# One dilated head moved beside another, a closing norm without GpSimd, and one root for four tiles

## The chip, the cores and the metric

One Trainium2 chip, one of its cores. The metric is the device time of one execution in microseconds (us). A core has five engines that run side by side: TensorE (PE in the profile; PEld are its weight loads), VectorE (DVE), ScalarE (ACT), GpSimd (POOL) and SyncE (SP), whose queue issues nearly all DMA transfers here. On-chip memory is SBUF (128 partitions) and PSUM (eight banks, where TensorE writes).

## What is computed

The reference runs two transformer blocks, one after the other, on 1024 tokens of width 1024. The first block (two attentions and a mixture of experts) ends about half way and is not touched. The second block, cut to what matters here:

```python
h = _rmsnorm(x, norm_attn_g) * (1.0 + sc1) + sh1              # opening norm
proj = h @ w_in
y_attn = _dilated_attention(q_a, k_a, v_a, rel_bias)           # 8 heads, three branches each
y_delta = _gated_deltanet(q_d, k_d, v_d, z_d, ...)             # 8 heads, a recurrence over chunks
x = x + g1 * (concatenate([y_attn, y_delta]) @ w_out)
h = _rmsnorm(x, norm_ffn_g) * (1.0 + sc2) + sh2
x = x + g2 * ((silu(h @ w_gate) * (h @ w_up)) @ w_down)
return _rmsnorm(x, final_norm_g)                               # closing norm
```

A norm is `x * rsqrt(mean(x*x) + eps) * g`. A dilated head has three branches: (window 128, dilation 1), (512, 4) and (2048, 16).

## The kernel before

Tokens are cut into eight tiles of 128 rows. Matrix products are done in three passes on operands split into a high and a low part (`mm3`). Each tile of data has a tag in a pool, and a pool has a number of buffers (`bufs`) for each tag; a new tile of a tag waits until an older one is released. A pool that is opened later may lie over the space of a closed one, and then its tiles wait for the old tiles under them. The order of the instructions on each engine is not written by hand: the framework (`TileContext(..., schedule_with_timeline_sim=True)`) replays a modelled timeline at build time and gives an engine whatever is ready in it, earlier program text first. On the chip each engine and the SP queue then run in that order.

**Opening norm** (`norm_rows`, L1381). The eight tiles are loaded (L2065) and normed in two groups of four, and each group in two pairs: ScalarE squares and sums each tile (L1390), `rsqrt_small` takes the root of the pair on VectorE in 13 small dependent instructions (L68 to L80), and VectorE and ScalarE scale one tile each (L1393). Then TensorE transposes the four tiles block by block (L1397), ScalarE applies the modulation (L1399), and the high and low parts are made (L1400, L1401; mostly VectorE).

**Dilated heads and recurrence** (`mix`, L1986). Heads 0 to 3 are computed earlier. Then come, in program text, the recurrence of the delta rule (L2145 to L2153; pool `t7` for its tiles, PSUM pool `psE` with two banks `dm` and one bank `ch`) and heads 4 to 7 (L2157). The heads use PSUM pool `psD`: two banks `sc` for scores, two banks `tr` for transposes, one bank `ov` for the product with the values. One head (`dilated_head`, L1524) goes through ten rounds: four of branch 1, four of branch 4, two of branch 16. A round is: score matmuls (L1529, L1530), bias and row minimum on VectorE (`soft`, L1533), exponential on ScalarE (L1534), transposes on TensorE (L1575, L1604 to L1606, L1630), a split into high and low parts that reads the transpose bank (`split`, L1543 to L1548), and the product with the values (`pv`, L1552 to L1554). Results leave through `dl_o2` (L1584) and `dl_on` (L1614, L1637; one buffer, so the third branch waits until the store of the second one, L1616, has landed). Heads 4 and 6 keep their operands in other places (`second`) than heads 5 and 7 (`t6`), but the biases `db1`, `db4`, `db16` have one place each, so that those of head 7 are loaded (L2039 to L2043) when head 6 has used its own. The working tiles (`dl_p`, `at_ph` and so on) are shared by all heads.

**After the heads** (`out_2`, L2163). The eight row blocks of `w_out` are loaded into three raw buffers (tag `big`, L2188), multiplied by the gate on GpSimd (L2189), and split by ScalarE and VectorE (L2190, L2191); the operands are split into `oA` (L2198, L2199), which lies over the operand places of head 7. In the program's memory layout the three raw buffers lie over the recurrence's `dt_nn` (bytes 59680 to 71967 of a partition against 62464 to 74751), and the split weights (`woh`, from byte 84512) lie over its `dt_wq`, `dt_z`, `dt_v` and `dt_zz`.

**Closing norm** (`ffn`, L2340 to L2354). The groups are tiles 0 to 2, 3 to 5, and 6 with 7. ScalarE squares, `rsqrt_small` takes the root, then an odd tile is scaled by VectorE in one instruction (L2350) and an even tile by ScalarE and GpSimd in two (L2352, L2353), and each tile is stored whole (L2354).

Of the kernel before, what the change touches and what calls it, by code (L numbers as in the profile page):

```python
# [6 lines left out]
F32 = mybir.dt.float32  # L7
F32R = mybir.dt.float32r
BF16 = mybir.dt.bfloat16
I32 = mybir.dt.int32  # L10
ALU = mybir.AluOpType
AF = mybir.ActivationFunctionType
AX = mybir.AxisListType
P = 128
T = 1024
D = 1024
# [4 lines left out]
EPS = 1e-6  # L21
# [10 lines left out]
class SplitPool:  # L32


    def __init__(self, a, na, b, nb):
        self.pools = [a] * na + [b] * nb
        self.n = {}

    def tile(self, shape, dt, tag=None, name=None, bufs=None):
        i = self.n[tag] = self.n.get(tag, -1) + 1  # L40
        return self.pools[i % len(self.pools)].tile(shape, dt, tag=tag, name=name)


class TagPool:
# [5 lines left out]
    def tile(self, shape, dt, tag=None, name=None, bufs=None):  # L50
        if tag in self.tags:
            pool, tag, bufs = self.tags[tag]
            return pool.tile(shape, dt, tag=tag, name=name, bufs=bufs)
        return self.main.tile(shape, dt, tag=tag, name=name, **({} if bufs is None else dict(bufs=bufs)))

# [7 lines left out]
def rsqrt_small(C, pool, out, x, n, scale, eps):  # L63

    nc = C.nc
    rows = x.shape[0]
    v = pool.tile([rows, n], F32, tag=f"rs_v{n}", name="rs_v")
    nc.vector.tensor_scalar(v, x, scale, eps, ALU.mult, ALU.add)  # L68
    i0 = pool.tile([rows, n], I32, tag=f"rs_i{n}", name="rs_i")
    nc.vector.tensor_scalar(i0, v.bitcast(I32), 1, None, ALU.logical_shift_right)  # L70
    y0 = pool.tile([rows, n], I32, tag=f"rs_y{n}", name="rs_y")
    nc.vector.tensor_scalar(y0, i0, -1.0, 1597463007.0, ALU.mult, ALU.add)
    nc.vector.tensor_scalar(v, v, -0.5, None, ALU.mult)
    y = y0.bitcast(F32)
    a = pool.tile([rows, n], F32, tag=f"rs_a{n}", name="rs_a")
    for it in range(3):
        nc.vector.tensor_mul(a, y, y)
        nc.vector.tensor_mul(a, a, v)
        dst = out if it == 2 else y
        last = nc.vector.scalar_tensor_tensor(dst, a, 1.5, y, ALU.add, ALU.mult)  # L80
    return last.ins
# [1299 lines left out]
def norm_rows(C, pool, xs, psp, a_col, s_col, ht):  # L1381

    nc = C.nc
    for g in range(2):
        for t2 in (4 * g, 4 * g + 2):
            ss = pool.tile([P, 2], F32, tag="nt_ss", name="nt_ss", bufs=2)
            rstd = pool.tile([P, 2], F32, tag="nt_r", name="nt_r", bufs=2)
            for j in range(2):
                junk = pool.tile([P, D], BF16, tag="nt_junk", name="nt_junk", bufs=2)
                nc.scalar.activation(junk, xs[t2 + j], AF.Square, accum_out=ss[:, j:j + 1])  # L1390
            rsqrt_small(C, pool, rstd, ss, 2, 1.0 / D, EPS)
            for j in range(2):
                (nc.scalar.mul if j else nc.vector.tensor_scalar_mul)(xs[t2 + j], xs[t2 + j], rstd[:, j:j + 1])  # L1393
        for k in range(KD):
            pt = psp.tile([P, 512], F32, tag=C.ps_tag, name="pt", bufs=C.ps_bufs)
            for j in range(4):
                nc.tensor.transpose(pt[:, j * P:(j + 1) * P], xs[4 * g + j][:, k * P:(k + 1) * P], C.ident)  # L1397
            full = pool.tile([P, 512], F32, tag="nt_full", name="nt_full", bufs=3)
            nc.scalar.activation(full, pt, AF.Identity, bias=s_col[:, k:k + 1], scale=a_col[:, k:k + 1])  # L1399
            (nc.scalar.copy if k % 4 == 3 else nc.vector.tensor_copy)(ht.hi[g][:, k], full)  # L1400
            nc.vector.tensor_sub(ht.lo[g][:, k], full, ht.hi[g][:, k])  # L1401
# [584 lines left out]
def mix(C, I, xtile, xclose, km, ext_d, c2_col, x2_d):  # L1986
    nc, tc = C.nc, C.tc
# [8 lines left out]
    num_d, f_d = mk("num_d", [3, 512, T]), mk("f_d", [3, 8, T])  # L1996
    yT_d = mk("yT_d", [512, T])
    w = I["w_in_2"][0]
    with ExitStack() as es:
# [31 lines left out]
                    yield  # L2031
        extra = iter(())

        def head(h, tp):
            qs = load_stack(C, tp, qa_d[h], "at_q")
            ks = load_stack(C, tp, ka_d[h], "at_k")
            kw = load_stack(C, tp, ka_d[h], "at_kw", swap=True)
            b1 = tp.tile([P, 256], F32, tag="db1", name="db1", bufs=1)
            nc.sync.dma_start(b1, toeplitz(ext_d, h, 0, P, 256, 127))  # L2039
            b4 = tp.tile([P, 256], F32, tag="db4", name="db4", bufs=1)  # L2040
            nc.sync.dma_start(b4, toeplitz(ext_d, h, 1, P, 256, 127))
            b16 = tp.tile([P, P], F32, tag="db16", name="db16", bufs=1)
            nc.sync.dma_start(b16, toeplitz(ext_d, h, 2, P, P, 255))  # L2043
            vh = va_d[:, h]
            v1 = tp.tile([P, NT, P], F32R, tag="dv1", name="dv1", bufs=1)
            nc.sync.dma_start(v1.bitcast(F32), vh.rearrange("(t p) c -> p t c", p=P))
            v4 = tp.tile([P, 4, 2, P], F32R, tag="dv4", name="dv4", bufs=1)
            v4s = vh.rearrange("(b j r) c -> j r b c", r=4, b=2)
            for r in range(4):
                nc.sync.dma_start(v4[:, r].bitcast(F32), v4s[:, r])  # L2050
            v16 = tp.tile([P, 8, P], F32R, tag="dv16", name="dv16", bufs=1)
            nc.sync.dma_start(v16.bitcast(F32), vh.rearrange("(j r) c -> j r c", r=8))
            dilated_head(C, tp, psp, qs, ks, kw, v1, v4, v16, b1, b4, b16, mn[:, h], rs[:, h], num_d, h,
                         lambda: next(extra, None))
        with ExitStack() as es2:
            ent2 = es2.enter_context
# [3 lines left out]
            with tc.tile_pool(name="t3", bufs=1, reuse_waits="tile") as tp:  # L2060
                ht = HT(C, ht_pool, "ht")
                xs = []
# [68 lines left out]
        with tc.tile_pool(name="t7", bufs=1, reuse_waits="tile") as td, \  # L2131
                tc.tile_pool(name="t8", bufs=1, reuse_waits="tile", side="right") as t8, \
                tc.tile_pool(name="psE", bufs=1, space=bass.MemoryType.PSUM, reuse_waits="tile") as psr:
            reserve(td, [("dt_yt", [P, 512], 2), ("dt_o", [P, 512], 2)])
            zs = []
            for nm in ("D", "V", "N"):
                zs.append([])
                for i in range(2):
                    z = td.tile([P, 8, P], F32, tag=f"z{nm}{i}", name="z" + nm)
                    nc.gpsimd.memset(z, 0.0)  # L2140
                    zs[-1].append(z)
            S = td.tile([P, 4, P], F32, tag="S", name="S")
            nc.gpsimd.memset(S, 0.0)
            inv, res = {}, {}
            for t in range(NT + 2):  # L2145
                if t < NT:
                    inv[t] = delta_inverse(C, td, psr, t, *zs, zT_d, U_d, T_d, V_d, qk_d, nat_d, qg_d)
                if 0 < t <= NT:
                    got = delta_chain(C, td, psr, t - 1, G, S, *inv.pop(t - 1))
                if t > 1:  # L2150
                    delta_out(C, td, psr, *res.pop(t - 2), yT_d)
                if 0 < t <= NT:
                    res[t - 1] = delta_sum(C, td, psr, *got)  # L2153
            second = TagPool(tp, dict(at_q=(posts, "cv_x", 2), at_k=(posts, "cv_x", 2), at_kw=(posts, "cv_y", 2),
                                      dv1=(posts, "cv_y", 2), dv4=(t8, "dv4", 1), dv16=(t8, "dv16", 1)))
            extra = first_half(TagPool(t8, dict(mr=(posts, "vp_nat", 2))))
            for h in range(4, 8):  # L2157
                head(h, second if h % 2 == 0 else tp)
        right.close()
    return dict(mn=mn, rs=rs, num_d=num_d, f_d=f_d, dil_d=dil_d, yT_d=yT_d, x2_d=x2_d)  # L2160

# [127 lines left out]
def ffn(C, I, y, ht, es, psp, out):  # L2289
    nc, tc = C.nc, C.tc  # L2290
# [10 lines left out]
    for g0 in range(0, NF, GS):  # L2301
# [30 lines left out]
        for t in range(NT):  # L2332
            st = slice(t * P, t * P + P)
            for nh in range(2):
# [2 lines left out]
                for f in fs:  # L2337
                    mm3(nc, ps, av[f][0][:, st], av[f][1][:, st], dw[f][0][:, ns], dw[f][1][:, ns], f == fs[0], f == fs[-1])
                nc.vector.tensor_add(y[t][:, ns], ps, y[t][:, ns])  # L2339
    for ts in ((0, 1, 2), (3, 4, 5), (6, 7)):  # L2340
        n = len(ts)
        ss = tp.tile([P, n], F32, tag="f_ss", name="f_ss", bufs=2)
        r = tp.tile([P, n], F32, tag="f_r", name="f_r", bufs=2)
        for j, t in enumerate(ts):
            junk = tp.tile([P, D], BF16, tag="sg", name="f_junk", bufs=2)
            nc.scalar.activation(junk, y[t], AF.Square, accum_out=ss[:, j:j + 1])
        rsqrt_small(C, tp, r, ss, n, 1.0 / D, EPS)
        for j, t in enumerate(ts):
            if t % 2:
                nc.vector.scalar_tensor_tensor(y[t], y[t], r[:, j:j + 1], fg, ALU.mult, ALU.mult)  # L2350
            else:
                nc.scalar.mul(y[t], y[t], r[:, j:j + 1])  # L2352
                nc.gpsimd.tensor_mul(y[t], y[t], fg)  # L2353
            nc.sync.dma_start(out[0, t * P:(t + 1) * P], y[t])  # L2354


def all_consts():
# [93 lines left out]
```

## Time and profile before

| what | us |
|---|---|
| median of 3 runs | 3562.4 |
| lowest and highest run | 3549.02, 3568.53 |
| the profiled execution, its own time | 3557.78 |
| its span, first to last instruction | 3556.0 |
| opening norm, first square to first product | 1885.65 to 1914.76 |
| heads 6 and 7, and what is left of the recurrence | about 2612 to 2685 |
| last `ps_dn` matmul of the kernel | about 3536.6 |

All times of rows are counted from the span's start. The span is one execution; its own time lies 1.78 us over its span and 4.6 us under the median. Busy shares are means over the whole span, so a stage is read from its own stretch.

### The profile page before, as it was taken

The page shows a single profiled execution, that of the slowest core. Times are in us where ns is not written, and L with a number is a line of the kernel's source. Part 1 is how long each engine was busy: PE and PEld are TensorE (multiplying, and loading weights), DVE is VectorE, ACT ScalarE, POOL GpSimd, SP SyncE. Part 2 cuts the span into 40 slices and gives each one's busy share as a digit, 9 for nine tenths or more (in the row PEclk, how much of TensorE's full clock was granted, in tenths as well). Part 3 has the DMA queues.
Part 4 walks back from the last instruction along what each step waited for, and adds up shares of the span by engine and source line. Part 5 has one row for each costly group of instructions (what it writes and reads, how often), then busy time and mean ns, then how long its engine had stood idle before and what let it go on. Part 6 is the DMA issues. An engine that isn't in the chain of part 4 may idle for free. (4 is left out here: it accounts for less than half of the span.)

```text
span 3556.0 us, 45053 instructions
## 1 busy us (share of the span) xinstructions
PE 3206.1 (90%) x15623; PEld 2529.3 (71%) x15623; DVE 2153.5 (61%) x4635; ACT 1408.2 (40%) x2610; POOL 705.3 (20%) x493
## 2 busy tenths in 40 slices
PE   7997898988879699999996988899998899999997
PEld 4866676766668466666665775688986788888886
DVE  5779895578657865666645676584776633333333
ACT  4345654555322344545434533265552311111112
POOL 0000033234242011111100000012233242322321
PEclk9998899998989799999997998899988999999999
DMA  6553535446564698999964566847665221111111
GB/s 202 124 163 83 156 115 160 132 143 202 178 204 165 252 304 320 336 336 343 332 218 148 155 202 212 195 139 222 181 189 187 68 77 42 54 48 42 54 36 48
DMA packets 442693, 601.38 MB, mean 169 GB/s; under 512 B 91081, under 2 KB 299097, under 8 KB 442464
## 3 DMA queue, kind: packets, MB, share of 16 engines
q1 hardware_dynamic: 433248, 581.17, 51.6%
q0 software_dynamic: 9216, 17.33, 2.0%
q8 instruction: 124, 2.03, 0.2%
q14 instruction: 105, 0.86, 0.1%
HBM read 498.78 MB, written 120.55 MB: 174 GB/s over the span
## 5 line engine op out<-in xcount | busy, mean ns | idle before, releaser
L246 ACT CAST wh<-wr 128x1024 fp32r<-128x1024 f32 (+1 forms) x392 | 379.2, 996 | 333.4 <-PE ps_gu L270 131.0
L250 DVE TENSOR_TENSOR wl<-wr,wh 128x1024 fp32r<-128x1024 f32 (+1 forms) x324 | 365.1, 1155 | 130.5 <-ACT wh L246 122.4
L269 PE MATMUL ps_gu<-hh,wh 128*128 128x512 f32 x704 | 274.7, 392 | 0.0
L270 PE MATMUL ps_gu<-hl,wh 128*128 128x512 f32 x704 | 274.1, 390 | 0.0
L271 PE MATMUL ps_gu<-hh,wl 128*128 128x512 f32 x704 | 273.9, 390 | 0.0
L269 PE MATMUL ps_feat<-hh,wh 128*128 128x512 f32 x640 | 266.6, 417 | 0.1
L270 PE MATMUL ps_feat<-hl,wh 128*128 128x512 f32 x640 | 261.1, 408 | 0.0
L271 PE MATMUL ps_feat<-hh,wl 128*128 128x512 f32 x640 | 260.7, 407 | 0.0
L1328 PE MATMUL ps_y<-wr,at 128*128 128x512 f32 x512 | 235.1, 614 | 24.9 <-ACT at L1322 24.9
L544 POOL TENSOR_TENSOR at_pl<-at_pf,at_ph 128x384 fp32r<-128x384 f32 (+1 forms) x96 | 91.6, 955 | 681.3 <-DVE at_ph L543 641.3
L2321 DVE TENSOR_TENSOR sg<-ps_gu,sg 128x512 f32<-128x512 f32 x44 | 30.4, 692 | 302.3 <-PE ps_gu L271 302.2
L269 PE MATMUL ps_e<-wh,xh 128*128 128x512 f32 x512 | 202.2, 402 | 1.2 <-ACT xh L1301 1.2
L2339 DVE TENSOR_TENSOR y<-ps_dn,y 128x512 f32<-128x512 f32 x176 | 120.7, 690 | 131.7 <-PE ps_dn L271 131.5
L270 PE MATMUL ps_e<-wl,xh 128*128 128x512 f32 x512 | 199.5, 397 | 0.0
L1328 PEld LDWEIGHTS ps_y<-wr,at 128*128 128x128 f32 x512 | 97.2, 195 | 143.0 <-issue 109.1
L271 PE MATMUL ps_e<-wh,xl 128*128 128x512 f32 x512 | 196.1, 397 | 2.4 <-DVE xl L1302 2.4
L250 POOL TENSOR_TENSOR wl<-wr,wh 128x1024 fp32r<-128x1024 f32 (+1 forms) x68 | 155.8, 2292 | 189.0 <-ACT wh L246 188.9
L161 DVE SCALAR_TENSOR_TENSOR adaacc<-adar,c,adaacc 128x512 f32<-128x512 f32 x140 | 118.6, 847 | 98.5 <-DMA adar<-in_w_ada 53.5
L526 ACT ACTIVATE at_p<-at_p,at_mn 128x128 f32<-128x128 f32 (+7 forms) x128 | 99.2, 776 | 185.9 <-DVE at_mn L524 185.7
L269 PE MATMUL ps_tok<-wh,hh 128*128 128x512 f32 (+2 forms) x448 | 169.7, 379 | 0.7 <-DVE hh L237 0.4
L270 PE MATMUL ps_tok<-wl,hh 128*128 128x512 f32 (+2 forms) x448 | 167.7, 374 | 0.0
L271 PE MATMUL ps_tok<-wh,hl 128*128 128x512 f32 (+2 forms) x448 | 166.7, 375 | 0.0
(622 smaller groups left out, 8175.2 us busy)
## 6 DMA issues: line engine op xcount, KB each, us to landing
wr<-in_exp_w SPq DMA_DIRECT2D x384, 512.0 KB
adar<-in_w_ada SPq DMA_DIRECT2D x96, 256.0 KB
wr<-in_w_in SPq DMA_DIRECT2D x44, 512.0 KB
adar<-in_ada_w SPq DMA_DIRECT2D x64, 256.0 KB
wr<-in_w_gate SPq DMA_DIRECT2D x22, 512.0 KB
wr<-in_w_up SPq DMA_DIRECT2D x22, 512.0 KB
dr<-in_w_down SPq DMA_DIRECT2D x22, 512.0 KB
wr<-in_w_in SPq DMA_DIRECT2D x40, 256.0 KB
```

Source lines behind the costliest of these rows:

```text
L161: nc.vector.scalar_tensor_tensor(acc, wt, c_col[:, k:k + 1], acc, ALU.mult, ALU.add)
L246: nc.scalar.copy(hi, raw)
L250: (nc.vector if eng[1] == "v" else nc.gpsimd).tensor_sub(lo, raw, hi)
L269: nc.tensor.matmul(out, sth, mvh, start=start, stop=False)
L270: nc.tensor.matmul(out, sth, mvl, start=False, stop=False)
L271: nc.tensor.matmul(out, stl, mvh, start=False, stop=stop)
L526: nc.scalar.activation(pr[:, :L], pr[:, :L], AF.Exp, bias=mn[:, nch - 1:nch], scale=-1.0, accum_out=rsum[:, qb:qb + 1])
L544: nc.gpsimd.tensor_sub(pl[:, off:], pf[:, off:], ph[:, off:])
L1328: nc.tensor.matmul(po, at[:, k], pcs2[k][:, ns], start=k == 0, stop=k == 3)
L2321: nc.vector.tensor_mul(s, pss[1], s)
L2339: nc.vector.tensor_add(y[t][:, ns], ps, y[t][:, ns])
```

## The change

Three edits. The opening norm takes one root for the four tiles of a group, and the squares of every second tile go to VectorE. Head 7 gets `work`, a pool that puts its working tiles into the places of the recurrence's tiles, and `banks`, which puts its scores and its transposes into the two `dm` banks and its value product into the `ch` bank; its operands and biases stay where they were. Its `dl_on` has two places in turn (`zD0`, `zV0`). The closing norm scales all tiles in one VectorE instruction each, tile 6 has its own root, and tile 7 is squared, scaled and stored in two halves.

```diff
+class CyclePool:
+    def __init__(self, main, tags):
+        self.main, self.tags, self.n = main, tags, {}
+    def tile(self, shape, dt, tag=None, name=None, bufs=None):
+        if tag in self.tags:
+            i = self.n[tag] = self.n.get(tag, -1) + 1
+            pool, tag, bufs = self.tags[tag][i % len(self.tags[tag])]
+            return pool.tile(shape, dt, tag=tag, name=name, bufs=bufs)
...
 (norm_rows)
-        for t2 in (4 * g, 4 * g + 2):
-            ss = pool.tile([P, 2], F32, tag="nt_ss", name="nt_ss", bufs=2)
...
-                nc.scalar.activation(junk, xs[t2 + j], AF.Square, accum_out=ss[:, j:j + 1])
-            rsqrt_small(C, pool, rstd, ss, 2, 1.0 / D, EPS)
+        for j in range(4):
+            junk = pool.tile([P, D], BF16, tag="nt_junk", name="nt_junk", bufs=2)
+            if j % 2:
+                nc.vector.scalar_tensor_tensor(junk, xs[4 * g + j], 1.0, xs[4 * g + j], ALU.mult, ALU.mult,
+                                               accum_out=ss[:, j:j + 1])
+            else:
+                nc.scalar.activation(junk, xs[4 * g + j], AF.Square, accum_out=ss[:, j:j + 1])
+        rsqrt_small(C, pool, rstd, ss, 4, 1.0 / D, EPS)
...
 (mix)
-            dilated_head(C, tp, psp, qs, ks, kw, v1, v4, v16, b1, b4, b16, mn[:, h], rs[:, h], num_d, h,
+            dilated_head(C, work or tp, banks or psp, qs, ks, kw, v1, v4, v16, b1, b4, b16, mn[:, h], rs[:, h], num_d, h,
...
-            for h in range(4, 8):
+            behind = lambda *tags: [(td, tag, bufs) for tag, bufs in tags]
+            work = CyclePool(td, dict(dl_p=behind(("dt_z", 3), ("dt_zz", 2), ("dt_u", 2)), at_ph=behind(("dt_v", 2)),
+                                      at_pl=behind(("dt_wq", 2)), dl_f=behind(("dt_vn", 2)), dl_p16=behind(("dt_nn", 2)),
+                                      dl_o2=behind(("dt_qk", 2)), dl_on=behind(("zD0", 1), ("zV0", 1))))
+            banks = TagPool(psp, dict(sc=(psr, "dm", 2), tr=(psr, "dm", 2), ov=(psr, "ch", 1)))
+            for h in range(4, 7):
                 head(h, second if h % 2 == 0 else tp)
+            head(7, tp, work, banks)
...
 (ffn)
-    for ts in ((0, 1, 2), (3, 4, 5), (6, 7)):
+    for ts in ((0, 1, 2), (3, 4, 5), (6,), (7,)):
+        n, parts = len(ts), 2 if ts == (7,) else 1
+        w = D // parts
...
+        if parts == 2:
+            nc.vector.tensor_add(ss[:, 0:1], ss[:, 0:1], ss[:, 1:2])
...
-            if t % 2:
-                nc.vector.scalar_tensor_tensor(y[t], y[t], r[:, j:j + 1], fg, ALU.mult, ALU.mult)
-            else:
-                nc.scalar.mul(y[t], y[t], r[:, j:j + 1])
-                nc.gpsimd.tensor_mul(y[t], y[t], fg)
-            nc.sync.dma_start(out[0, t * P:(t + 1) * P], y[t])
+            for q in range(parts):
+                c = slice(q * w, (q + 1) * w)
+                nc.vector.scalar_tensor_tensor(y[t][:, c], y[t][:, c], r[:, j:j + 1], fg[:, c], ALU.mult, ALU.mult)
+                nc.sync.dma_start(out[0, t * P:(t + 1) * P, c], y[t][:, c])
```

## Rows read from the trace of the kernel before

**Rows 1.** The page: busy time by engine, and the chain's shares by engine.
```profile
PE 3206.1 (90%) x15623; PEld 2529.3 (71%) x15623; DVE 2153.5 (61%) x4635; ACT 1408.2 (40%) x2610; POOL 705.3 (20%) x493
...
PE 31%; DMA 6%; DVE 6%; ACT 1%; issue 1%; SPq 1%; POOL 0%; POOLq 0%; DVEq 0%; ACTq 0%
```

**Rows 2.** Stretches, opening norm: length, PE, PEld, DVE, ACT, POOL busy, clock, DMA.
```profile
1885.00:1897.00 12.00, 3.35 (x12) 2.15 (x12) 7.22 (x42) 10.89 (x19) 0.00 (x0) 0.50 1.05 394
1897.00:1909.00 12.00, 7.51 (x28) 5.13 (x29) 12.00 (x31) 11.06 (x15) 0.00 (x0) 0.50 0.34 91
```

**Rows 3.** Order in time on ScalarE, opening norm: start, duration, instruction, idle before.
```profile
1889.56 1.06 ACT L1390 ACTIVATE nt_junk<-wr 128x1024 bf16<-128x1024 f32 x1
...
1896.85 1.43 ACT L1399 ACTIVATE nt_full<-pt,sh,a 128x512 f32<-128x512 f32 x2
```

**Rows 4.** Order in time on VectorE: first and last instruction of one root.
```profile
1888.12 0.17 DVE L68 TENSOR_SCALAR rs_v<-nt_ss 128x2 f32<-128x2 f32 x1 [13.47 <-DMA wr<-x_d]
...
1890.30 0.16 DVE L80 SCALAR_TENSOR_TENSOR nt_r<-rs_a,rs_y 128x2 f32<-128x2 f32 x1
```

**Rows 5.** Busy time by stretch, heads 6 and 7 (columns as in Rows 2).
```profile
2629.00:2685.00 56.00, 47.77 (x326) 43.86 (x326) 38.52 (x122) 36.77 (x112) 27.40 (x20) 0.80 0.55 170
2671.00:2685.00 14.00, 7.55 (x65) 6.25 (x66) 10.40 (x11) 7.74 (x11) 6.25 (x5) 0.81 0.33 90
```

**Rows 6.** The chain that ended last, in time, where head 7 ends.
```profile
2678.39 2.90 DMA num_d<-dl_on
...
2683.55 3.71 DMA wr<-in_w_out
```

**Rows 7.** Order in time on TensorE, last value products of head 7.
```profile
2678.42 0.28 PE L1552 MATMUL po<-dl_ph,dv 128*64 128x128 f32 x1 [1.63 <-ACT dl_on L1614]
...
2682.53 0.37 PE L1552 MATMUL po<-dl_ph,dv 128*64 128x128 f32 x1 [3.17 <-DVE dl_on L1637]
```

**Rows 8.** Order in time on the SP queue: head 7's biases, branches 1 and 16.
```profile
2624.99 0.90 SPq L2039 DMA_DIRECT2D db<-ext_d  x1
...
2645.01 0.32 SPq L2043 DMA_DIRECT2D db<-ext_d  x1
```

**Rows 9.** Order in time: head 7's first reduction, then a later round.
```profile
2644.90 0.29 DVE L1533 CUSTOM_DVE_ANT_0 dl_p<-ps_d,db 128x128 f32<-128x128 f32 x1
...
2651.59 0.51 PE L1575 MATMUL pt<-ident,dl_p 128*128 128x128 f32 x3
...
2651.86 0.36 PE L1529 MATMUL ps_d<-at_k,at_q 128*128 128x256 f32 x1
...
2652.96 0.42 DVE L1533 CUSTOM_DVE_ANT_0 dl_p<-ps_d,db 128x256 f32<-128x256 f32 x1
...
2653.48 0.56 DVE L1548 TENSOR_TENSOR dl_pl<-pt,dl_ph 128x384 fp32r<-128x384 f32 x1
```

**Rows 10.** Order in time on GpSimd, the gate on one row block.
```profile
2687.39 2.48 POOL L2189 TENSOR_TENSOR wr<-wr,g1b 128x1024 f32<-128x1024 f32 x1 [7.88 <-DMA wr<-in_w_out]
```

**Rows 11.** Order in time on VectorE, closing norm.
```profile
3534.51 1.83 DVE L70 TENSOR_SCALAR rs_i<-rs_v 128x3 int32<-128x3 int32 x1
...
3541.69 2.30 DVE L68 TENSOR_SCALAR rs_v<-f_ss 128x2 f32<-128x2 f32 x1
...
3546.20 1.29 DVE L2350 SCALAR_TENSOR_TENSOR y<-y,f_r,fgb 128x1024 f32<-128x1024 f32 x1
```

**Rows 12.** The chain that ended last, in time, closing norm.
```profile
3540.76 3.21 POOL y L2353
...
3547.45 2.38 POOLq L2447
```

**Rows 13.** Busy time by stretch, closing norm (columns as in Rows 2).
```profile
3524.00:3537.00 13.00, 12.58 (x56) 10.09 (x54) 10.99 (x28) 7.56 (x12) 4.80 (x2) 1.00 0.20 81
3537.00:3556.00 19.00, 0.00 (x0) 0.00 (x0) 9.86 (x26) 3.33 (x4) 5.54 (x2) 0.58 0.42 166
```

**Rows 14.** Order in time on the SP queue, the eight stores.
```profile
3531.73 18.45 SPq L2354 DMA_DIRECT2D out<-y  x8
```

More of the change, by code (lines that the diff above doesn't have):

```diff
@@ L52, in tile @@
             pool, tag, bufs = self.tags[tag]
+            return pool.tile(shape, dt, tag=tag, name=name, bufs=bufs)
+        return self.main.tile(shape, dt, tag=tag, name=name, **({} if bufs is None else dict(bufs=bufs)))
+class CyclePool:
[5 more added lines that the diff above has]
+            pool, tag, bufs = self.tags[tag][i % len(self.tags[tag])]
             return pool.tile(shape, dt, tag=tag, name=name, bufs=bufs)
@@ L1384, in norm_rows @@
     for g in range(2):
-        for t2 in (4 * g, 4 * g + 2):
-            ss = pool.tile([P, 2], F32, tag="nt_ss", name="nt_ss", bufs=2)
-            rstd = pool.tile([P, 2], F32, tag="nt_r", name="nt_r", bufs=2)
-            for j in range(2):
-                junk = pool.tile([P, D], BF16, tag="nt_junk", name="nt_junk", bufs=2)
-                nc.scalar.activation(junk, xs[t2 + j], AF.Square, accum_out=ss[:, j:j + 1])
-            rsqrt_small(C, pool, rstd, ss, 2, 1.0 / D, EPS)
-            for j in range(2):
-                (nc.scalar.mul if j else nc.vector.tensor_scalar_mul)(xs[t2 + j], xs[t2 + j], rstd[:, j:j + 1])
+        ss = pool.tile([P, 4], F32, tag="nt_ss", name="nt_ss", bufs=2)
+        rstd = pool.tile([P, 4], F32, tag="nt_r", name="nt_r", bufs=2)
+        for j in range(4):
[6 more added lines that the diff above has]
+        rsqrt_small(C, pool, rstd, ss, 4, 1.0 / D, EPS)
+        for j in range(4):
+            (nc.scalar.mul if j % 2 else nc.vector.tensor_scalar_mul)(xs[4 * g + j], xs[4 * g + j], rstd[:, j:j + 1])
         for k in range(KD):
@@ L2032, in mix, with head @@
         extra = iter(())
-        def head(h, tp):
+        def head(h, tp, work=None, banks=None):
             qs = load_stack(C, tp, qa_d[h], "at_q")
@@ L2339, in ffn @@
                 nc.vector.tensor_add(y[t][:, ns], ps, y[t][:, ns])
-    for ts in ((0, 1, 2), (3, 4, 5), (6, 7)):
-        n = len(ts)
-        ss = tp.tile([P, n], F32, tag="f_ss", name="f_ss", bufs=2)
+    for ts in ((0, 1, 2), (3, 4, 5), (6,), (7,)):
+        n, parts = len(ts), 2 if ts == (7,) else 1
+        w = D // parts
+        ss = tp.tile([P, n * parts], F32, tag="f_ss", name="f_ss", bufs=2)
         r = tp.tile([P, n], F32, tag="f_r", name="f_r", bufs=2)
         for j, t in enumerate(ts):
-            junk = tp.tile([P, D], BF16, tag="sg", name="f_junk", bufs=2)
-            nc.scalar.activation(junk, y[t], AF.Square, accum_out=ss[:, j:j + 1])
-        rsqrt_small(C, tp, r, ss, n, 1.0 / D, EPS)
-        for j, t in enumerate(ts):
-            if t % 2:
-                nc.vector.scalar_tensor_tensor(y[t], y[t], r[:, j:j + 1], fg, ALU.mult, ALU.mult)
-            else:
-                nc.scalar.mul(y[t], y[t], r[:, j:j + 1])
-                nc.gpsimd.tensor_mul(y[t], y[t], fg)
-            nc.sync.dma_start(out[0, t * P:(t + 1) * P], y[t])
+            for q in range(parts):
+                junk = tp.tile([P, w], BF16, tag="sg", name="f_junk", bufs=2)
+                nc.scalar.activation(junk, y[t][:, q * w:(q + 1) * w], AF.Square, accum_out=ss[:, j + q:j + q + 1])
+        if parts == 2:
+            nc.vector.tensor_add(ss[:, 0:1], ss[:, 0:1], ss[:, 1:2])
+        rsqrt_small(C, tp, r, ss[:, 0:n], n, 1.0 / D, EPS)
+        for j, t in enumerate(ts):
+            for q in range(parts):
+                c = slice(q * w, (q + 1) * w)
+                nc.vector.scalar_tensor_tensor(y[t][:, c], y[t][:, c], r[:, j:j + 1], fg[:, c], ALU.mult, ALU.mult)
+                nc.sync.dma_start(out[0, t * P:(t + 1) * P, c], y[t][:, c])
 def all_consts():
```

## The prediction

> **What bounds the kernel now.** First the page: TensorE is busy 90% of the span, and the largest share of the chain that ended last, 31%, is its own [rows 1]. That invites the reading that only TensorE's work counts, and none of the three edits removes TensorE work. So the next view is the busy time by stretch, at the places of the edits.
>
> In the opening norm TensorE is busy 3.35 of 12 us at first [rows 2]; the reader is to see that ScalarE (10.89 of 12, then 11.06) leads and VectorE (7.22, then 12.00) takes over. The bound here is the chain from the loads through squares, root and scaling to the first transposed part. In heads 6 and 7 TensorE is busy 47.77 of 56 us: it leads, with 8.23 us idle, of which 6.45 lie in the last 14 us [rows 5]. The order in time on TensorE says what the idle time there is: 1.63 and 3.17 us ahead of the last value products [rows 7], and the chain says why: a store of `dl_on` of 2.90 us that the third branch waits for [rows 6]. In the closing norm TensorE is busy 12.58 of 13 us and then not at all for 19 us [rows 13]; whatever shortens those 19 us shortens the run one for one.
>
> **Opening norm.** Removed: four of eight ScalarE squares of 1.06 us [rows 3] and two of four roots. A root is 13 dependent operations from 1888.12 to 1890.46, 2.34 us [rows 4]. Added: four squares on VectorE. No such instruction is in the rows; the nearest is the scaling of the same form and size, 1.29 us [rows 11], and I take 1.25, with 1.06 (ScalarE's) and 1.46 (as far above) as bounds. Chain for the first group: the fourth tile's square can start at 1889.56, as now [rows 3]; 1.25 on VectorE ends at 1890.8, the root at 1893.2, and two scalings on each engine, at ScalarE's 1.06 a tile, at about 1895.3. Some 0.5 for the last tile's transpose, and the first transposed part is taken up at 1895.8; now it is at 1896.85 [rows 3]. So I take −1.0. If the removed root's whole 2.34 comes off, −2.3; if the framework puts two VectorE squares of the second group (2 x 1.25) into the first group's root, +2.5. VectorE, at 12.00 of 12 later in the stage, is why I don't take the full gain. The shift carries into the first product, which waits for the group's transposes.
>
> **Heads 6 and 7.** Nothing is removed; a dependency is. Head 7 now begins when head 6's last scores leave the banks, at 2644.90 [rows 9]. Its first bias (one place, free since head 6 used its own) is issued from 2624.99 on for 0.90 [rows 8]; with a transfer of 2.90 like the store's [rows 6] it has landed at 2628.8. The recurrence has left its banks by about then, so 2629 is the earliest start. The bias of branch 16 was issued at 2645.01 [rows 8], and still needs head 6's to be used first: only branches 1 and 4 can move much. TensorE's work is the same. What can be won is idle time: 8.23 us [rows 5]. With two heads to draw on and two places of `dl_on` I fill all of it: −8.2. Of the clock the row says 0.80 granted [rows 5], so 40% of the stretch at 1.2 GHz and the rest at 2.4. Fewer gaps may raise it; I take 0.86, 47.77 x (1 − 0.80/0.86) = −3.3, with bounds 0.80 (0) and 0.92 (−6.2).
>
> On the other side, the places move a cost downstream. The raw buffers of `w_out` lie over `dt_nn`, where head 7 keeps `dl_p16` until its end, and the split weights over its other places. Before, three row blocks are loaded and gated ahead of head 7's end; after, they follow it. Each is 2.48 us on GpSimd [rows 10], so up to 7.4 us is uncovered, plus a load of 3.71 [rows 6] that other loads overlap. But the fourth block's load starts only at 2683.55 even now [rows 6], and the product needs the six following blocks too; head 7 ends earlier by the gain, and the blocks catch up. I take +2, bounds 0 and +7.4. The SP queue carries head 7's stores and then these loads; an earlier head moves both.
>
> The banks: head 7 has two for scores and transposes where the others have four. Score start to last reduction's end is 2651.86 to 2653.38, 1.5 us; transposes to the split's end 2651.59 to 2654.04, 2.45 us [rows 9]. Taken in turn, each kind has one bank, so rounds cannot be closer than 2.45: ten are 24.5 us, 2629 to 2654, ahead of the bias of branch 16 or near it. So the banks cost nothing while they only take turns; fully serial, 4.0 us a round, is the rival below. Sum: −8.2 − 3.3 + 2 = −9.5, rounded to −9; bounds −14.4 (−8.2 − 6.2) and, from the rival, +11.
>
> **Closing norm.** Removed: GpSimd's scalings, 3.21 on the chain and 2.38 just before its last link [rows 12], and ScalarE's. VectorE stalls while GpSimd runs: 1.83 and 2.30 us [rows 11] for small root operations of 0.17 elsewhere [rows 4], 3.8 us together. Added on VectorE: four scalings of 1.29 [rows 11], one root (2.3 us alone, about 1.5 among other work) and one small add. VectorE is busy 10.99 + 9.86 = 20.85 us in the last 32 us [rows 13]; 20.85 − 3.8 + 5.2 + 1.6 = 23.8. It was idle half of the last 19 us, so it has room, but becomes the tail's bound. After the last addition, at about 3537, the new path is a half square (half of ScalarE's 1.06, twice, overlapped with the product's end), add, root 2.3, two half scalings of 0.65, and a half store. VectorE's queue ends at 3546.5 to 3548.4; now the last store is issued at 3550.18, the end of the eight stores' group [rows 14], and lands 5.8 us later. So the issue comes 2 to 3.5 us earlier and the half-size store lands perhaps 0.7 earlier: −3.5; bounds −5.5 (VectorE's 23.8 without a gap, from 3524) and −0.5 (every saved microsecond queued on VectorE).
>
> [...] The row that carries the largest term is TensorE's 47.77 busy of 56, with weight loads at 43.86 in the same stretch [rows 5]. [...]
>
> **The rivals.** Sum for the forecast: −1.0 − 9 − 3.5 = −13.5 on the profiled 3557.78, or 3544.3; that execution is 4.6 us under the median, and the run is compared with medians, so 3549.
> - *Forecast*, 3543 to 3555.
> - *A: more room on TensorE.* Its records overlap, so a busy stretch can take more. For: weight loads leave 12.1 us [rows 5]. Against: both rows count the same 326 instructions on one array, and a matmul's own time is part of it. −1.0 − (12.1 + 3.3 − 2) − 3.5 = −17.9: 3544.5; with the clock's bounds 3541 to 3548.
> - *B: slower.* Place: the two `dm` banks. Scores and transposes of one round hold both and the next waits for the whole round: 4.0 us unloaded, and in a stretch where TensorE and VectorE serve two heads 1.4 times that, 5.6. It decides from 5.2 us a round on, (2685 − 4 − 2629)/10: head 7 then ends no earlier than now. At 5.6 it ends 4 later, and the uncovered gating of `w_out` adds 7.4: +11.4 − 4.5 = +6.9, 3569; at 7 us a round 3583. For: `dl_p` rounds hold banks through VectorE, busy 38.5 of 56, and ScalarE, 36.8 [rows 5]. Against: the two kinds take turns, as said.
> - *C: the gain goes.* Head 7 starts early, but what ends the stretch stays: the branch of dilation 16 waits for its bias, and the gated weights come as late as now. Heads 0, other edits −4.5: 3558. For: the fourth block at 2683.55 [rows 6]. Against: the 4.8 us of waits [rows 7] go in any case.
>
> The Trainium skill ("Perfetto Trace Analysis", section "Optimizing Tensor Performance") says that independent matmul groups should rotate through different PSUM banks so that emptying one overlaps the next; head 7 rotates through half as many, which is B's side, and by it the time would be B's 3569.
>
> **How the numbers follow.** Chances: forecast 0.42, A 0.25, B 0.19, C 0.14. The predicted time is 3549. The range: from 3533 (every term at its best: −2.3 − 14.4 − 5.5 = −22.2 gives 3540, and the run spread of before reaches 13 us under its median, of which I take half) to 3573 (B's 3569 and some). About 0.07 lies below, 0.10 above. 0.5% is 17.8 us, about what a measurement of this kernel can tell from no change, as single runs spread over 19.5 us. Faster means under 3544.6: of the forecast 0.3 of its chance (its lower end and the spread), of A most (0.8): 0.33. Slower means over 3580: B's far end, 0.09. Same: 0.58.
>
> **What would show it.** Head 7's first reduction near 2630 and not 2644.9; its last store before 2680; the waits of 1.63 and 3.17 gone; a stretch 2629 to 2675 with TensorE busy over 93% and a granted clock over 0.80; the `w_out` loads bunched behind head 7. Against: reductions of head 7 over 5 us apart (B), or the first products of `out_2` where they were (C). Opening: the first modulated part near 1895.9. Tail: no GpSimd, no VectorE operation of 0.17 that takes 2 us, last store issued near 3547, 16 us from the last product to the end where it was 19.4. The prediction fails if the replayed order, which every edit changes, puts other work ahead in stages between 1900 and 3524 that no edit touches.

## The result and the profile after

The changed kernel takes 3582.6 us (median of 10), the kernel before 3555.6 in the runs beside it: ratio 1.0082, 95% interval 1.0070 to 1.0094. It is slower by 27 us (medians) or 29 (the ratio); the prediction said 3549 and left 0.09 for slower. Its profiled execution has a span of 3582.4 us, 26.4 more than before.

The page after, busy time by engine and the chain's shares, beside [rows 1]:

```profile
PE 3211.2 (90%) x15623; PEld 2532.3 (71%) x15623; DVE 2163.3 (60%) x4636; ACT 1403.2 (39%) x2600; POOL 695.7 (19%) x489
...
PE 31%; DMA 7%; DVE 6%; issue 2%; ACT 1%; SPq 1%; POOL 1%; DVEq 0%; POOLq 0%; ACTq 0%
```

TensorE has the same 15,623 instructions and 5 us more busy time: 21 of the 26 us are idle time. Where it lies is read by cutting both spans at six landmarks: the first square of the opening norm, the first product `ps_tok`, the first product of the recurrence (`ps_z`), the last output tile of the recurrence (`dt_yt`), the last evacuation of head 7 (`dl_on`), and the last `ps_dn`. Each entry is the difference of two such times, in us:

| stretch | before | after | change |
|---|---|---|---|
| opening norm | 29.1 | 32.2 | +3.1 |
| to the recurrence | 511.0 | 509.8 | −1.2 |
| recurrence (with heads 4 to 6) | 222.5 | 229.2 | +6.7 |
| rest of heads 6 and 7 | 36.9 | 45.6 | +8.7 |
| end of the heads to the last product | 851.3 | 870.3 | +19.0 |
| closing norm | 19.4 | 14.7 | −4.7 |

The remaining −5.0 lies ahead of the first square (1885.7 before, 1880.7 after), in work that no edit touches. Busy time by stretch after, for head 7, for what follows it, and for the end (length, PE, PEld, DVE, ACT, POOL, granted clock, DMA), beside [rows 5, 13]:

```profile
2651.00:2697.00 46.00, 35.36 (x212) 29.17 (x211) 20.83 (x65) 24.89 (x76) 11.86 (x10) 0.71 0.30 82
2697.00:2709.00 12.00, 2.20 (x14) 1.43 (x13) 2.35 (x3) 3.11 (x5) 3.82 (x2) 0.64 0.82 282
3555.00:3568.00 13.00, 12.75 (x57) 10.23 (x55) 11.39 (x27) 5.42 (x9) 0.00 (x0) 1.00 0.30 121
3568.00:3582.40 14.40, 0.00 (x0) 0.00 (x0) 10.86 (x46) 1.53 (x6) 0.00 (x0) 0.63 0.46 182
```

Head 7 leaves TensorE idle for 10.6 of 46 us at a granted clock of 0.71, and behind the head TensorE works 2.2 of 12 us. VectorE's order in time, head 7's first and last reductions after, beside the first line of [rows 9]:

```profile
2651.16 0.67 DVE L1999 TENSOR_TENSOR dt_yt<-pt_y,dt_z 128x512 f32<-128x512 f32 x1
2651.76 0.27 DVE L1550 CUSTOM_DVE_ANT_0 dl_p<-ps_d,db 128x128 f32<-128x128 f32 x1
...
2684.31 0.29 DVE L1550 CUSTOM_DVE_ANT_0 dl_p<-ps_d,db 128x128 f32<-128x128 f32 x1 [2.57 <-PE ps_d L1547]
...
2689.03 0.28 DVE L1550 CUSTOM_DVE_ANT_0 dl_p<-ps_d,db 128x128 f32<-128x128 f32 x1
```

Head 7 doesn't start earlier: its first reduction stands right behind the recurrence's last `dt_yt`, which reads the last output tile, transposed into `pt_y`, out of a `dm` bank. TensorE, in order of time there:

```profile
2649.99 0.60 PE L1997 MATMUL pt_y<-ident,dt_o 128*128 128x128 f32 x4
2650.35 0.31 PE L1546 MATMUL ps_d<-at_k,at_q 128*128 128x128 f32 x1
```

Head 7's first scores come right behind the transposes `pt_y`, and before `dt_yt` reads these out (2651.16), so they go into the other `dm` bank. The recurrence's last tile there, `ps_i`, had been read by 2632.46: that bank had been empty for some 18 us. So no full bank held head 7; its place in TensorE's order, behind `pt_y`, did, and why the framework put it there isn't shown. And from its first to its last reduction it takes 37.6 us; before it took 23.2 (2644.90 to 2668.13). The SP queue after, behind the head:

```profile
2697.46 0.45 SPq L1655 DMA_DIRECT2D num_d<-dl_on  x1
2697.95 0.58 SPq L2201 DMA_DIRECT2D g1b<-rg  x1
...
2699.26 0.39 SPq L2211 DMA_DIRECT2D wr<-in_w_out  x1
```

The first load of `w_out` is issued 1.8 us behind head 7's last evacuation; before it was issued 30.1 us ahead of it (2655.14 against 2685.25). TensorE after, in order of time:

```profile
2696.12 2.73 PE L1669 MATMUL pt_w<-ident,dmn 128*4 128x128 f32 x16
2708.65 1.65 PE L283 MATMUL ps_o<-woh,oA 128*128 128x512 f32 x3 [9.80 <-ACT woh L2213]
```

It waits 9.80 us for the first split block. So about half of the 19 us is lost before the first product ends, 12.0 us behind the head where it was 2.1. The other half builds up over the stage: loads, gates and splits that lay under head 7 now stand beside the products, and the first transposes of the next norm come 121.0 us behind the head where they came at 102.9. Groups of instructions on VectorE, 2697 to 2733 after (busy us, mean ns of one):

```profile
L2222 DVE TENSOR_TENSOR oA<-mo,oA 128x512 fp32r<-128x512 f32 x8 | 12.5, 1583 | 11.4 <-ACT oA L2221 11.4
L2214 DVE TENSOR_TENSOR wol<-wr,woh 128x1024 fp32r<-128x1024 f32 x6 | 9.8, 1633 | 0.6 <-ACT woh L2213 0.6
```

A split of `oA` takes 1583 ns in the mean where its undisturbed ones take 690, since GpSimd's gating runs beside it. VectorE is full from 2712 to 2728, the evacuations of `pt_w` come behind the splits, and the dilated weights are stored at 2757.2, 59.8 us behind the head; before it was 42.3. The chain that ended last goes through these weights.

### The profile page after: what moved, and what is told of

It reads as the page before. It is cut to its first block, busy times and chain, and to the rows that moved or that the text cites. A ratio compares the mean times of both kernels' runs of the same rounds, so it can differ in the third digit from the quotient of the medians.

```text
span 3582.4 us, 45023 instructions
## 1 busy us (share of the span) xinstructions
PE 3211.2 (90%) x15623; PEld 2532.3 (71%) x15623; DVE 2163.3 (60%) x4636; ACT 1403.2 (39%) x2600; POOL 695.7 (19%) x489
## 5 line engine op out<-in xcount | busy, mean ns | idle before, releaser
L2344 DVE TENSOR_TENSOR sg<-ps_gu,sg 128x512 f32<-128x512 f32 x44 | 30.4, 692 | 302.8 <-PE ps_gu L285 302.3
```

## The experiments

All ratios are to the kernel before on the same chip, and differences in us are the ratio times its median there. For each run the same stretches were cut; the table behind the runs has them.

**The edits one by one.** The first three each take the functions of one edit into the kernel before: `ffn`; `norm_rows`; `mix` with `CyclePool`. The fourth is the changed kernel with `head(7, tp)`.

> The kernel before with the closing norm of the changed kernel alone. Theory 1 (the three edits add up, and the loss is all in heads 6 and 7 and behind them): 4 to 6 us faster, as in the changed kernel's trace, where the span from the last product of the kernel to its end is 14.7 us and was 19.4. Theory 2 (the gain there is only the state in which the late kernel arrives): within 2 us of the kernel before.

Measured 3542.4 against 3548.9 us, 0.9982 (0.9971 to 0.9993): 6.4 us faster. Theory 1 holds for this edit.

> The kernel before with the opening norm of the changed kernel alone. Theory 1: the edit itself costs about 3 us from the first square to the first product (in the changed kernel's trace 32.2 us, before 29.1), and nothing else, so +3. Theory 2 (the other replayed order): the recurrence and heads 4 to 6 come another 8 to 10 us later, as in the changed kernel, where its last chunk is 7 us late: +10 or more. Theory 3 (no effect): within 2 us.

3559.0, 1.0028 (1.0015 to 1.0042): 9.9 us slower, as theory 2 has it. Opening norm 31.3 us, recurrence 231.3.

> The kernel before with head 7's places and banks of the changed kernel alone. Theory 1: +28, since the two other edits give +3 and -5 and the whole kernel is 27 us slower. Theory 2 (the opening edit's order): +18 or less, and the recurrence is not late.

3573.4, 1.0070 (1.0057 to 1.0083): 24.8 us slower, the recurrence as before (221.0). That is nearer theory 1.

> The changed kernel with head 7 in the old banks and places. Theory 1: -1 to -3 (the sum of +3 and -5). Theory 2 (the opening edit's order costs the recurrence time): +4 or more.

3552.5, 1.0007 (0.9997 to 1.0017): +2.5, about what −6.4 and +9.9 make. And 0.9982 x 1.0028 x 1.0070 = 1.0080 against 1.0082 measured: the edits add up.

**The head's two halves.**

```diff
-            head(7, tp, work, banks)
+            head(7, tp, None, banks)      # banks alone
+            head(7, tp, work)             # places alone
```

> The kernel before with head 7 in the recurrence's three banks, its working tiles in the old places. Theory 1 (the two halves of the move cost separately): ten rounds of head 7 take 35 to 40 us where they took 24, the head ends some 10 us later, but the weights of w_out are loaded under it, so TensorE has no 10 us hole behind the head: +8 to +13. Theory 2 (only the banks matter; what follows is late because the head is late): +20 to +25, like the whole head edit. Theory 3 (only the places matter): within 3 us.

3563.3 against 3545.9, 1.0042 (1.0032 to 1.0052): +14.9. Head 7's reductions take 36.1 us; the loads of `w_out` start 45 us ahead of its end, and the stretch behind it is 851.4 us, as before.

> The kernel before with head 7's working tiles in the recurrence's places and two places for its last results, its banks the old ones. Theory 1: rounds at the old 2 us, the head ends up to 5 us earlier, the loads of w_out begin only behind its last store and TensorE then waits some 10 us: +5 to +13. Theory 2 (only the banks matter): -5 to +2. Theory 3 (only the places matter): +20 to +25.

3572.8, 1.0063 (1.0042 to 1.0085): +22.3. Reductions in 23.4 us, the head's end about as before (35.4 us), and 870.5 us behind it. So each half costs by itself, and the places more than theory 1 had expected. They don't add up (15 and 22 against 25): with the new places the slow head ends 43.6 us behind the recurrence, with the old ones 50.9.

**Two places for `dl_on` alone.**

```diff
-            head(7, tp, work, banks)
+            head(7, tp, CyclePool(tp, dict(dl_on=behind(("zD0", 1), ("zV0", 1)))))
```

> The kernel before with two places for the last results of head 7 (over two tiles of the recurrence that nothing after the head needs soon) and nothing else moved. If the waits of 1.63 and 3.17 us at the end of head 7 are on the path that counts: 3 to 5 us faster. If the fourth block of w_out and the operands of the next stage are what ends the stretch: within 2 us.

3557.3, 1.0027 (1.0014 to 1.0041): 9.6 us slower, which neither theory had.

> The two places for the last results of head 7 together with the closing norm of the changed kernel: if the two gains add, 8 to 11 us faster than before; if the first is nothing, 5 to 6.5 faster as the closing norm alone.

3554.5, 1.0023 (1.0009 to 1.0036): +8.2, which neither of the two had. The rest of the heads is shorter in both (34.3 and 31.6 us, 36.9 before), yet the stretch behind it is 870 and 871 us. TensorE's two waits at the end of head 7, with the two places alone, beside [rows 7]:

```profile
2652.25 0.27 PE L1566 MATMUL po<-dl_ph,dv 128*64 128x128 f32 x1 [1.63 <-ACT dl_on L1628]
...
2654.34 0.37 PE L1566 MATMUL po<-dl_ph,dv 128*64 128x128 f32 x1 [1.16 <-DVE dl_on L1651]
```

The first is the same 1.63 us as before: it ends when ScalarE has copied the product out of the one `ov` bank, and a second place for `dl_on` doesn't touch that. The second falls from 3.17 to 1.16 us. So what waited for the store is 2.0 of the 4.8 us. The SP queue in the same kernel:

```profile
2657.02 0.45 SPq L1652 DMA_DIRECT2D num_d<-dl_on  x1
2657.52 0.99 SPq L2198 DMA_DIRECT2D g1b<-rg  x1
...
2659.04 0.46 SPq L2208 DMA_DIRECT2D wr<-in_w_out  x1
```

No tile of the next stage that is loaded here lies over `zD0` or `zV0` (35840 to 39935 and 44032 to 48127; `g1b` and the raw buffers lie from 55584 on), and still all loads stand behind the last store. So it isn't the bytes under a tile that hold them. In the built program the load of `g1b` and the first three of `w_out` wait for no instruction of head 7; only their place in the queue, behind its last store, holds them. So it is the order, which puts the next stage's first tile over the recurrence's pool behind the last use of that pool. To test it, the first place is the head's own `dl_on` again and the second goes into another pool:

```diff
+            head(7, tp, CyclePool(tp, dict(dl_on=[(tp, "dl_on", 1), (t8, "dv4", 1)])))
```

> As the kernel with two places for the last results of head 7, but the second place lies where head 6's values of branch 4 were, outside the recurrence's pool. Theory 1 (the order given to the SP queue: a tile of the recurrence's pool that head 7 still uses puts every load of the next stage behind head 7's last store, which cost about 19 us in each of the four kernels that did it): the loads of w_out start about 2655 again, the head still ends some 8 us earlier, so 4 to 9 us faster than before, and 14 or more faster than the kernel with the places in the recurrence's pool (+9.7 measured). Theory 2 (the loads are late because head 7 ends early and the order follows): loads behind the last store, about +10 again.

3557.6 against 3560.0, 0.9994 (0.9981 to 1.0007): not to be told from no change, and some 12 us better than with both places in the recurrence's pool. The SP queue here:

```profile
2663.13 0.46 SPq L1630 DMA_DIRECT2D num_d<-dl_on  x1
2663.93 0.33 SPq L2198 DMA_DIRECT2D g1b<-rg  x1
...
2665.07 0.43 SPq L2208 DMA_DIRECT2D wr<-in_w_out  x1
...
2692.54 0.45 SPq L1652 DMA_DIRECT2D num_d<-dl_on  x1
```

The loads go ahead of the last store by 27 us, and the stretch behind the head is 852.8. Theory 1 holds for the loads; its 4 to 9 us of gain don't show.

> The same with the closing norm of the changed kernel. By theory 1 the gains add: 9 to 15 us faster than before (6.5 of it from the closing norm). By theory 2: +2 to +5.

3552.4, 0.9980 (0.9965 to 0.9994): 7.1 us faster, short of the 9 to 15 of theory 1, and not to be told from the closing norm alone.

**The opening edit's halves.** One root for four with ScalarE's squares, and VectorE's squares with a root for each pair:

```diff
-            if j % 2:
-                nc.vector.scalar_tensor_tensor(junk, ...)
-            else:
-                nc.scalar.activation(junk, ...)
+            nc.scalar.activation(junk, ...)
```

> The opening norm with one root for four tiles, all squares on ScalarE as before. Theory 1 (the common root costs: no tile of a group is scaled before its last square): first square to first product 31 to 33 us (before 29.1). Theory 2 (the squares on VectorE cost, since they stand in the root's chain): 29 to 30 us. For the whole kernel both leave open what the changed order does to the recurrence; +0 to +12.

3571.5, 1.0037 (1.0021 to 1.0054): +13.2; opening norm 30.6 us.

> The opening norm with the squares of every second tile on VectorE and a root for each pair as before. Theory 1: first square to first product 28 to 29.5 us, no loss. Theory 2: 31 us or more. Whole kernel: -2 to +2 if the recurrence's order stays, +5 to +10 if it changes as in the kernel with the whole opening edit.

3568.8, 1.0023 (1.0010 to 1.0036): +8.2; opening norm 32.9 us. The squares lengthen the opening, as theory 2 has it; the common root does so less, by 1.5 us, which lies between the two theories (kernels with the old opening differ by 0.8). Both halves together take 31.3 us (the opening alone), so the halves don't add. For the common root most of the 13.2 us come from elsewhere; for the squares the stretches can't say, as the profiled execution is 10 us faster than that kernel's median.

**The order, and the banks again.** TensorE's instructions come in the old order, from the recurrence's first product to its last transposes, in every kernel above with the old `norm_rows` (at most 2 of 1,793 differ); in those that touch it 830 to 879 stand elsewhere. So one operation of no use is added to the old one, at a root where the order stays, or where it changes:

```diff
             rsqrt_small(C, pool, rstd, ss, 2, 1.0 / D, EPS)
+            if t2 == 2:    # and in the next run t2 == 6
+                nc.vector.tensor_scalar_mul(rstd, rstd, 1.0)
```

> The kernel before with one more VectorE operation (the root times 1.0, 0.17 us) behind the second root of the opening norm; the order of TensorE's instructions in the recurrence is that of before. Theory A and B: within 2 us of before.

3546.2 against 3546.5, 1.0005 (0.9991 to 1.0019).

> The same operation behind the last root of the opening norm instead; this changes the replayed order in the recurrence. Theory A (the order costs): +4 to +10. Theory B: within 2 us.

3547.9, 1.0012 (0.9998 to 1.0026): +4.3, with no change just inside the interval; 879 instructions elsewhere. Neither theory is helped.

> Two such operations behind each of the last two roots, 0.7 us at most on VectorE, and another order again. Theory A: a change well beyond 0.7 us, +4 to +10 if orders other than that of before tend to be worse. Theory B: 0 to +1.

3563.2, 1.0043 (1.0027 to 1.0060): 15 us for operations of 0.7 us at most; recurrence 230.6 us, 830 instructions elsewhere. Theory A holds: a new order can cost 15 us, and need not.

The two new orders are ones met before. From the first product `ps_tok` to the end of the heads, TensorE has the same order with the four operations as with one root for four, and the same with the one operation as with the squares on VectorE. So the +13.2 of the common root stands beside +15.2 for no useful work: its order carries it. The squares' +8.2 stands beside +4.3, and the 3.9 between them is about the 3.1 us by which their opening is longer. The order of the whole opening edit was not run with a useless operation.

The last run moves only the transposes of head 7 into the `dm` banks:

```diff
+            head(7, tp, None, TagPool(psp, dict(tr=(psr, "dm", 2))))
```

> The kernel before with only the transposes of head 7 in the recurrence's two banks; scores and value products in the old ones, working tiles in the old places. Theory A (sharing two banks is what slows the rounds): ten rounds in 20 to 26 us as before, and the whole within 4 us. Theory B: 30 us or more, and +8 or more.

3547.2, 0.9996 (0.9984 to 1.0007). Reductions in 23.7 us. Busy time from first to last reduction, here and (second fence) with both kinds in the `dm` banks:

```profile
2642.36:2666.00 23.64, 21.41 (x144) 19.81 (x143) 13.31 (x58) 18.10 (x64) 10.92 (x8) 0.80 0.74 244
```

```profile
2642.43:2678.50 36.07, 29.63 (x176) 24.73 (x174) 20.06 (x65) 20.94 (x60) 17.35 (x12) 0.72 0.57 185
```

TensorE is idle 2.2 of 23.6 us with four banks and 6.4 of 36.1 with two, at a lower granted clock. The second kernel also has its value product in the `ch` bank; that, and the scores alone in the `dm` banks, were not run apart.

| run | opening | recurrence | rest of heads | behind | closing | ratio |
|---|---|---|---|---|---|---|
| closing alone | 29.2 | 221.2 | 37.9 | 851.5 | 14.7 | 0.9982 |
| opening alone | 31.3 | 231.3 | 40.7 | 852.9 | 19.4 | 1.0028 |
| opening and closing | 31.3 | 226.1 | 40.1 | 852.5 | 14.6 | 1.0007 |
| head alone | 29.2 | 221.0 | 43.6 | 870.2 | 19.4 | 1.0070 |
| banks alone | 29.0 | 221.8 | 50.9 | 851.4 | 19.4 | 1.0042 |
| places alone | 29.8 | 220.5 | 35.4 | 870.5 | 19.4 | 1.0063 |
| `dl_on` twice, `t7` | 29.1 | 216.8 | 34.3 | 870.1 | 19.4 | 1.0027 |
| the same and closing | 29.1 | 220.5 | 31.6 | 871.4 | 14.8 | 1.0023 |
| `dl_on` twice, `t8` | 29.1 | 222.7 | 33.3 | 852.8 | 19.5 | 0.9994 |
| the same and closing | 29.0 | 220.4 | 38.3 | 851.3 | 14.7 | 0.9980 |
| one root for four | 30.6 | 223.3 | 40.0 | 856.2 | 19.4 | 1.0037 |
| squares on VectorE | 32.9 | 217.6 | 38.7 | 849.3 | 19.4 | 1.0023 |
| one operation, old order | 29.0 | 222.3 | 36.8 | 851.2 | 19.4 | 1.0005 |
| one operation, new order | 29.8 | 217.0 | 38.9 | 850.6 | 19.4 | 1.0012 |
| four operations, new order | 30.4 | 230.6 | 40.1 | 858.7 | 19.4 | 1.0043 |
| transposes moved alone | 29.2 | 221.6 | 39.9 | 851.0 | 19.4 | 0.9996 |

## Why the prediction was wrong

**Heads 6 and 7: −9 forecast, +24 measured (head alone 24.8), and five steps failed.**

The first is the earliest start, "2629". It came from the first bias, as if a landed bias and an empty bank were enough. The bias was issued at 2629.24 in the trace after, and of the two `dm` banks one was empty from 2632.46 on; head 7's scores still came at 2650.35, right behind the transposes `pt_y` in TensorE's order. In the three kernels with head 7 in the recurrence's banks (banks alone, head alone, after) its first reduction begins 0.07 to 0.09 us ahead of the end of the last `dt_yt`. With the old score banks it is 2.9 to 3.4 us ahead where the opening norm is the old one. The gain of the idle time rested on the early start.

The second is "the banks cost nothing while they only take turns". The rounds would then be 2.45 us apart; ten take 36 to 37.6 us, near the 4.0 a round that stood in rival B. The runs come close to showing that mechanism: with the transposes alone moved, 23.7 us and no loss; with scores and transposes in the two banks and the value product in `ch`, 36.1 us. The Trainium skill ("Perfetto Trace Analysis", section "Optimizing Tensor Performance") asks that independent groups rotate through different PSUM banks; the two runs agree, 23.7 us against 36.1. Rival B mis-sized its price: it held for a head that begins at 2629 and let it end 4 us late, and it ended 8.7 later in its stretch, 14.0 with the banks alone.

The third and largest is the term of +2 for `w_out`, bounds 0 and +7.4: it is 19.0 us. I counted the gating of three blocks and let the rest catch up. What I took for a wait of single tiles, a raw buffer over `dl_p16`, is a place in an order: where head 7 uses places of pool `t7`, the next stage's loads come behind its last store, five kernels of five at 870 to 871 us (head alone, places alone, `dl_on` twice with and without the closing norm, and the changed kernel), and those without it at 849 to 853, or 856 and 859 in two with new orders. The fourth is the idle time, −8.2, with the 4.8 us of waits at its end. The prediction read both waits as the store's, and rival C says that they go in any case. Of the 4.8 us only 2.0 go with two places for `dl_on`; the 1.63 us is the one `ov` bank. In the four kernels with two places and the old banks TensorE is idle 5.0 to 8.8 of the last 56 us of the head, where before it was 8.2. So none of the four filled more than 3.2 of the 8.2 us.

The fifth is the clock, −3.3 for a rise from 0.80 to 0.86. In the changed kernel head 7 has 0.71 (2651 to 2697). In the two kernels with the second place in `t8`, which have one order on TensorE, the last 56 us of the head have 0.93 and 0.80, and the rest of the heads takes 33.3 and 38.3 us. So the clock differs more between two such executions than the term was to bring, and the whole time shows no gain that can be told.

Rival A, more room on TensorE, never came to a test, since head 7 didn't start early.

**Opening norm: −1.0 forecast, +3.1 in its stretch and 10 in the run alone.** VectorE after, in order of time, and TensorE's wait, beside [rows 3, 4]:

```profile
1886.87 0.17 DVE L82 TENSOR_SCALAR rs_v<-nt_ss 128x4 f32<-128x4 f32 x1
...
1888.15 1.22 DVE L1404 SCALAR_TENSOR_TENSOR nt_junk<-wr 128x1024 bf16<-128x1024 f32 x1
...
1890.08 0.16 DVE L94 SCALAR_TENSOR_TENSOR nt_r<-rs_a,rs_y 128x4 f32<-128x4 f32 x1
...
1892.94 0.17 DVE L82 TENSOR_SCALAR rs_v<-nt_ss 128x4 f32<-128x4 f32 x1
...
1904.00 0.16 DVE L94 SCALAR_TENSOR_TENSOR nt_r<-rs_a,rs_y 128x4 f32<-128x4 f32 x1
```

```profile
1905.57 2.79 PE L1414 MATMUL pt<-ident,wr 128*128 128x128 f32 x12 [5.54 <-DVE wr L1410]
```

The square is sized right (1.22, estimated 1.25). The first group's step failed in part: its first modulated part comes 12.9 us behind the first square, where it came at 11.2 and 10.2 was forecast. Of that 2.7 us, 1.0 is one square of the next group inside the root, which takes 3.37 us (the bound that I had named, +2.5, was for two); the rest is a third tile that landed about 1.0 late in this execution, and 0.7 between the root and the part. What I left out is the second group: its root, 2.34 us alone, takes 11.2 among other VectorE work, and since it is one root, none of its four tiles can be scaled before; TensorE waits 5.54 us. ScalarE's first scaling there begins at 1904.19, 23.5 us behind the first square; before, with a root for the pair, at 1899.84, 14.2 us behind it. The step worked out the first group's chain alone. The common root isn't the whole cause: alone it leaves a wait of 4.06 us there, and with a root for each pair and VectorE's squares TensorE waits 3.31 us in the first group and 2.97 in the second, and that opening is longer still (32.9).

The other 7 us of the edit aren't in its stretch. In the recurrence the same edit gives 231.3, 226.1 and 229.2 us in its three kernels, and the old order 220 to 223 (216.8 once). One useless operation shows that a new order may also be free there (217.0). With four it takes 230.6, and 223.3 in the common root's kernel, which has the same order: a stretch of one execution scatters by some 7 us, and the whole time (1.0043) is the firmer number. That the order, not the work, carries this part is shown for the common root's order, and supported for the order of the whole edit; which instruction in it is the costly one isn't found.

**Closing norm: −3.5 forecast, −4.7 in its stretch, −6.4 (−2.5 to −10.3) in the run alone.** Right, and within the bounds. VectorE after, in order of time, beside [rows 11], and then the SP queue, beside [rows 14]:

```profile
3570.69 3.68 DVE L2378 SCALAR_TENSOR_TENSOR y<-y,f_r,fgb 128x1024 f32<-128x1024 f32 x3
...
3577.79 1.41 DVE L2378 SCALAR_TENSOR_TENSOR y<-y,f_r,fgb 128x512 f32<-128x512 f32 x2
```

```profile
3562.91 16.66 SPq L2379 DMA_DIRECT2D out<-y  x9
```

Counted from the last product, 3567.75, the last issue ends at +11.8, for +13.6 before: −1.8, close to the 2 to 3.5 forecast. From there to the span's end it is 2.8 us where it was 5.8. Of these 3.0 the half store gives about 0.6, as forecast (0.7): the last packet ends 1.4 us behind the issue, before 1.9. The other 2.4 lie between the last packet and the span's end, 1.5 us where it was 3.9, and the prediction had no term for them; their cause isn't shown. The roots' operations take 0.14 to 0.17 us, with no stall of 2 us. The Trainium skill ("SBUF — State Buffer", section "Who interferes with whom") calls the port pair of VectorE and GpSimd an exclusive lock; the trace agrees, 1.83 and 2.30 us beside GpSimd's scalings [rows 11], 0.17 without.

The closing norm alone, 0.9982, beats both kernels.

## What to carry to other kernels

Before lending a pool's places to a later piece of work, ask what is allocated over that pool next: here one tile with two borrowed places held a whole stage's loads, for 19 us, though none of these loads lay over it. An empty bank and landed operands don't make work start early: here the engine's order did not let it. Two kinds of tile that alternated in two banks took 36 us for rounds that took 24 with two banks each. Where a tool orders the instructions, run each edit alone, beside a useless operation that gives the same order, before the edit's own cost is believed.

## What was unexpected

Operations of 0.7 us in all, far from the recurrence, changed the time by 15 us with the order. And with one order the stretch from the first product to the recurrence took from 503.3 to 517.3 us in kernels that don't differ there; the median of the kernel before was 3546 to 3560 us in the four sets of runs, so ratios were taken within a set.
